# Softmax transposes of an attention stage as two 64-row halves in place of one 128-row block

## Chip, cores and metric

The kernel runs on one core of a Trainium2 chip. The metric is device time in microseconds (us), the median of repeated executions. Engines are named as the profile names them: PE is TensorE's matmul, PEld its weight load, DVE VectorE, ACT ScalarE, POOL GpSimd, SP SyncE.

## The reference

One layer of an encoder trunk, sequence length 1024, width 1024, all in float32. Cut to what matters here:

```python
hn = rmsnorm(h, norm_mix_g); z = hn @ w_in
u, (q, k, v) = z[..., :512], jnp.split(z[..., 512:], 3, axis=-1)   # 8 heads of 64
a = pool_mixer(u, pool_w, pool_b, pool_scale)
o = chunk_attention(q, k, v, rel_bias)       # own chunk of 64 and the 8 before it
h = h + jnp.concatenate([a, o], -1) @ w_out
# then a gated MLP with a causal convolution (d_ff 2816), a gated per-layer embedding, a last rmsnorm

# inside chunk_attention, for one chunk of 64 queries
s = jnp.einsum('bqhd,bkhd->bhqk', qb, kb) * scale + bias
pr = jax.nn.softmax(jnp.where(valid, s, -inf), axis=-1)
out = jnp.einsum('bhqk,bkhd->bqhd', pr, vb)
```

## The kernel before

Every large product is made of three matmuls on halves of a float32 number (`mm3`, lines 126 to 130: high by high, high by low, low by high); `split` (lines 132 to 134) makes the halves with one ACT copy and one DVE subtraction. These products fill almost the whole program.

The attention stage handles 64 tiles `i`, 8 heads by 8 blocks of 128 queries. A block sees `nk` blocks of 128 keys: 1, 2, 3, 4 and then 5 for the last four blocks of a head, so the stage has 8 x (1+2+3+4+4x5) = 240 blocks of probabilities. For each tile:

- `scores(i)` (lines 333 to 361): scores on PE into banks 4 and 5 of PSUM; DVE adds the bias and finds the row extreme (L346 for five blocks, L354 for fewer); ACT takes the exponential with a row sum (L356); DVE takes the reciprocal (L357); ACT (L359) or DVE (L361) scales. The probabilities stand in `S`, in tile `F`, queries on the partitions, float32.
- `probs_t(i)` (lines 363 to 378), two tiles later: the `nk` blocks of `S` are transposed on PE (L370) so that keys stand on the partitions. The results go to PSUM banks 6 and 7 (`pst`), from which ACT writes the high half (L377) and DVE the low half (L378) to the tile `PT`, which lies in `B`. There is one `pst`: the first transpose of a tile waits until L378 of the tile before has read it.
- `values` (lines 380 to 394), every second tile: probabilities by values (L387, L388) and their evacuation (L393, L394).

A transpose here loads the block of `S` as the array's weights (LDWEIGHTS, stationary) and streams the identity `ident` through it (MATMUL, moving): the output block has as many columns as the moving operand.

PE's order is the order in which the code is written. Between the attention's own matmuls the loop puts steps of a generator `rest()`: one `mm3` of the input projections of later heads and of the pooling part. `fill_room` and `credit` set how many such steps go to each tile. The order on DVE and ACT is set by a scheduler by priorities; the evacuations L377 and L378 are asked for early (`tc.high_priority(AHEAD)`).

The stage runs from about 60 us to 282 us of the span; the first and last L370 start at 60.5 and 268.5 us. Output projection, MLP and the rest follow.

Of the kernel before, what the change touches and what calls it, by code (L numbers as in the profile page):

```python
# [11 lines left out]
P = 128  # L12
# [5 lines left out]
HD = 64  # L18
# [75 lines left out]
def trunk(tc, xT, pT, vecs, w_qk0, w_in, w_v, bias, counts, pool_w, w_out, w_up, w_down,  # L94
          w_gate, w_ple, out):
    nc = tc.nc
    act, dve, pe, pool, sp = nc.scalar, nc.vector, nc.tensor, nc.gpsimd, nc.sync

    with tc.tile_pool(name="sb", bufs=1) as sb, \
# [7 lines left out]
        ident = sb.tile([P, P], F32, name="ident")  # L107
        PS = pp.tile([P, 8, 512], F32, name="PS")
# [6 lines left out]
        def r(kb, n):  # L115
            if kb >= 128:
                return B[:, int((kb - 128) * KW):int((kb - 128) * KW) + n]
            return R[:, int(kb * KW):int(kb * KW) + n]
# [4 lines left out]
        def rv(ap):  # L123
            return ap.bitcast(F32)
# [203 lines left out]
        def keys(i):  # L328
            t = i % NTOK
            k0 = max(0, t - 4)  # L330
            return i // NTOK, t, k0, t + 1 - k0
# [31 lines left out]
        def probs_t(i):  # L363
            h, t, k0, nk = keys(i)
            S = Sb[i % 3]
            w = i // 2
            pt = PT[w % 2]
            pst = PS[:, 6:8].rearrange("p a b -> p (a b)")[:, 0:nk * P]
            for j in range(nk):
                pe.transpose(pst[:, j * P:(j + 1) * P], S[:, j * P:(j + 1) * P], ident)  # L370
            pst = pst.rearrange("p (k q) -> p k q", k=nk)
            i0 = k0 - (t // 2 * 2 - 4)
            qs = slice(t % 2 * P, (t % 2 + 1) * P)
            hi = pt[:, 0, i0:i0 + nk, qs]
            lo = pt[:, 1, i0:i0 + nk, qs]
            with tc.high_priority(AHEAD):
                act.activation(hi, pst, AF.Copy)  # L377
                dve.tensor_tensor(lo, pst, rv(hi), ALU.subtract)  # L378
# [162 lines left out]
        for i in range(NI + 3):  # L541
            if i < NI:
                h, t, k0, nk = keys(i)
# [15 lines left out]
            for z in range(n_):  # L559
                if due and z >= n_ // 2:  # L560
                    probs_t(i - 2)
                    due = False
                if next(fill, True) is False:
                    break
                credit -= 1
            if due:
                probs_t(i - 2)
# [189 lines left out]
        for z, d in enumerate((0, 4, 1, 5, 2, 6, 3, 7)):  # L757
            k = z // 2
# [297 lines left out]
        pt = [[(r(b, 512), r(b + 2, 512)) for b in (96 + 16 * h, 104 + 16 * h)] for h in range(2)]  # L1056
# [238 lines left out]
```

## Time and profile before

| | |
|---|---|
| median of 3 runs | 1137.39 us (1137.12 to 1137.82) |
| the profiled execution's own time | 1137.53 us |
| its span, first to last instruction | 1135.8 us |
| granted TensorE clock, mean | 0.998 of full speed |
| PE busy in the span | 99% |
| DVE, ACT busy in the span | 78%, 53% |
| transposes L370 | 240 matmuls, 240 weight loads |

Rows of a timeline give the start, the length, the engine, the line, the operation and what it writes and reads; runs of the same instruction are merged with a count. TensorE's matmuls overlap, and a row's length is longer than the distance to the next start; the work of one is best read from that distance. In rows of groups the numbers behind the bar are the group's total busy time in us, the mean of one in ns, and the idle time of the engine before them.

### The profile page before, as it was taken

What the parts mean: (1) busy time and instruction counts of PE and PEld (TensorE: products, weight loads), DVE (VectorE), ACT (ScalarE), POOL (GpSimd) and SP (SyncE); (2) the same over time, 40 slices, a digit from 0 to 9 for tenths busy, and PEclk for the clock granted to TensorE, in tenths of its full rate; (3) what the DMA queues carried; (4) which work ended last, traced back from release to release, by engine and by line L of the source; (5) the groups of instructions that cost most, each with busy time, mean ns of one, the idle gap of its engine ahead of it and who ended that gap; (6) DMA issues with size and microseconds to landing.
All of it is one profiled execution on the core that took longest, in us unless ns stands there. A gap on an engine that the chain in (4) does not pass through costs nothing.

```text
span 1135.8 us, 15750 instructions
## 1 busy us (share of the span) xinstructions
PE 1126.1 (99%) x5675; PEld 956.0 (84%) x5675; DVE 891.0 (78%) x1546; ACT 604.5 (53%) x1071; POOL 143.1 (13%) x188
## 2 busy tenths in 40 slices
PE   9999999999999999999999999999999999999997
PEld 7988998888888888888888888888888888888897
DVE  7678878779658888887788778877887789986854
ACT  8568677765654554444444444444444444674544
POOL 0000000074002200120112011201120112000000
PEclk9999999999999999999999999999999999999999
DMA  7110102103600154575557555755575556420012
GB/s 267 38 50 31 49 13 68 40 29 131 194 19 10 57 151 135 139 174 142 137 155 178 143 130 162 176 145 131 159 171 151 130 152 129 147 93 19 1 75 75
DMA packets 64446, 124.84 MB, mean 110 GB/s; under 512 B 7280, under 2 KB 8560, under 8 KB 64368
## 3 DMA queue, kind: packets, MB, share of 16 engines
q1 hardware_dynamic: 50400, 98.60, 25.9%
q0 software_dynamic: 13824, 25.17, 13.6%
q8 instruction: 44, 0.72, 0.3%
q14 instruction: 34, 0.28, 0.1%
q10 hardware_dynamic: 144, 0.07, 0.0%
HBM read 109.13 MB, written 14.68 MB: 109 GB/s over the span
## 4 chain that ended last, share of the span: by engine, by line
PE 92%; DVE 3%; issue 2%; ACT 1%; POOL 1%; DMA 0%; SPq 0%; POOLq 0%; DVEq 0%; ACTq 0%
PE PS L128 28%; PE PS L129 28%; PE PS L130 28%; PE PS L370 2%; PE PS L388 1%; PE PS L387 1%; DVE R L134 1%; PE PS L345 1%; PE PS L344 1%; ACT R L133 1%; DMA F<-in_w_qk 0%; PE PS L353 0%; PE PS L352 0%; POOL TB L778 0%; DVE F L760 0%
## 5 line engine op out<-in xcount | busy, mean ns | idle before, releaser
L128 PE MATMUL PS<-R 128*128 128x512 f32 (+1 forms) x1176 | 442.7, 376 | 0.2 <-ACT R L232 0.2
L130 PE MATMUL PS<-R 128*128 128x512 f32 (+1 forms) x1176 | 437.8, 372 | 0.0
L129 PE MATMUL PS<-R 128*128 128x512 f32 (+1 forms) x1112 | 420.1, 378 | 0.3 <-DVE R L233 0.3
L130 PEld LDWEIGHTS PS<-R 128*128 128x128 f32 x1176 | 221.7, 188 | 39.0
L128 PEld LDWEIGHTS PS<-R 128*128 128x128 f32 x1176 | 221.8, 189 | 37.8 <-ACT R L232 0.6
L129 PEld LDWEIGHTS PS<-R 128*128 128x128 f32 x1112 | 209.7, 189 | 37.0 <-DVE R L233 0.8
L133 ACT ACTIVATE R<-F 128x512 fp32r<-128x512 f32 (+2 forms) x225 | 140.6, 637 | 173.9 <-PE PS L129 75.2
L134 DVE TENSOR_TENSOR R<-F,R 128x512 fp32r<-128x512 f32 (+2 forms) x221 | 152.8, 701 | 48.3 <-ACT R L133 47.5
L1013 DVE TENSOR_TENSOR F<-F,PS 128x512 f32<-128x512 f32 x140 | 92.6, 682 | 5.8 <-PE PS L130 5.6
L133 ACT ACTIVATE BQ<-RW 128x512 fp32r<-128x512 f32 x90 | 52.6, 622 | 81.1 <-PE PS L129 77.1
L703 DVE TENSOR_TENSOR F<-F 128x512 f32<-128x512 f32 x88 | 60.7, 689 | 39.0 <-DMA F<-in_w_up 37.2
L956 POOL DMA_DIRECT2D RW<-Yd x56 | 49.0, 875 | 260.3 <-DMA RW<-Yd 201.4
L956 POOL DMA_DIRECT2D RW<-in_w_down x40 | 35.5, 941 | 233.5 <-DMA RW<-in_w_down 189.7
L134 DVE TENSOR_TENSOR BQ<-RW,BQ 128x512 fp32r<-128x512 f32 x90 | 59.2, 687 | 1.8 <-PE PS L129 1.3
L356 ACT ACTIVATE F<-F,small 128x640 f32<-128x640 f32 (+2 forms) x64 | 44.4, 693 | 21.3 <-DVE small L354 13.2
L129 PE MATMUL PS<-BQ 128*128 128x512 f32 x140 | 54.6, 390 | 0.1
L130 PE MATMUL PS<-BQ 128*128 128x512 f32 x140 | 54.5, 389 | 0.0
L128 PE MATMUL PS<-R,BQ 128*128 128x512 f32 x140 | 54.5, 389 | 0.0
L128 PE MATMUL PS<-BQ 128*128 128x512 f32 x140 | 54.5, 389 | 0.0
L129 PE MATMUL PS<-R,BQ 128*128 128x512 f32 x140 | 54.5, 389 | 0.0
L130 PE MATMUL PS<-R,BQ 128*128 128x512 f32 x140 | 54.5, 389 | 0.0
L839 ACT ACTIVATE F<-F,vec 128x1024 f32<-128x1024 f32 (+1 forms) x25 | 28.6, 1143 | 44.2 <-DVE F L814 40.8
(188 smaller groups left out, 1806.3 us busy)
## 6 DMA issues: line engine op xcount, KB each, us to landing
F<-in_w_up SPq DMA_DIRECT2D x91, 256.0 KB, 4.0
RW<-Yd SPq DMA_DIRECT2D x60, 256.0 KB, 3.7
RW<-Yd POOLq DMA_DIRECT2D x56, 256.0 KB, 4.8
RW<-in_w_down SPq DMA_DIRECT2D x50, 256.0 KB, 2.8
RW<-in_w_down POOLq DMA_DIRECT2D x40, 256.0 KB, 6.0
Yd<-F SPq DMA_DIRECT2D x40, 256.0 KB, 3.1
F<-in_w_in SPq DMA_DIRECT2D x10, 512.0 KB, 3.7
F<-in_xT SPq DMA_DIRECT2D x16, 256.0 KB, 5.8
```

Source lines behind the costliest of these rows:

```text
L128: pe.matmul(ps, ahi, bhi, start=first, stop=False, skip_group_check=more)
L129: pe.matmul(ps, ahi, blo, start=False, stop=False, skip_group_check=more)
L130: pe.matmul(ps, alo, bhi, start=False, stop=last, skip_group_check=more)
L133: both = (act.activation(hi, src, AF.Copy), dve.tensor_tensor(lo, src, rv(hi), ALU.subtract))
L134: dve.tensor_tensor(lo, src, rv(hi), ALU.subtract))
L344: pe.matmul(PS[:, 4 + z, 0:320], q, K2[:, ks], start=True, stop=False)
L356: act.activation(S[:, 0:n], S[:, 0:n], AF.Exp, bias=s_[:, 0:1], scale=-1.0, accum_out=s_[:, 1:2])
L370: pe.transpose(pst[:, j * P:(j + 1) * P], S[:, j * P:(j + 1) * P], ident)
L703: return dve.tensor_tensor(rawu[to], rawu[a], rawu[b], op)
L839: act.activation(y, Gb[:, 2 + a:2 + b], AF.Identity, bias=vec[:, C_CB + fi:C_CB + fi + 1], scale=cw(2))
L956: pool.dma_start(t, src, accum_op=ALU.add)
L1013: dve.tensor_tensor(t, t, PS[:, 4 + d], ALU.subtract if n in (1, 5) else ALU.add)
```

## The change

Each transpose of 128 queries by 128 keys becomes two of 64 queries by 128 keys. The first takes partitions 0 to 63 of `S` and the upper left quarter of `ident` and stands on the upper 64 rows of the array; the second takes partitions 64 to 127 and the lower right quarter and stands on the lower 64 rows (`tile_position`). Each writes 64 columns instead of 128, the first to bank 6 and the second to bank 7. The two evacuations read both banks in turns of 64 columns and write the same places as before.

```diff
-            pst = PS[:, 6:8].rearrange("p a b -> p (a b)")[:, 0:nk * P]
             for j in range(nk):
-                pe.transpose(pst[:, j * P:(j + 1) * P], S[:, j * P:(j + 1) * P], ident)
-            pst = pst.rearrange("p (k q) -> p k q", k=nk)
+                for x in range(2):
+                    rows = slice(HD * x, HD * x + HD)
+                    pe.transpose(PS[:, 6 + x, j * HD:(j + 1) * HD], S[rows, j * P:(j + 1) * P], ident[rows, rows],
+                                 tile_position=(HD * x, 0))
+            pst = PS[:, 6:8, 0:nk * HD].rearrange("p a (k q) -> p k a q", k=nk)
             i0 = k0 - (t // 2 * 2 - 4)
             qs = slice(t % 2 * P, (t % 2 + 1) * P)
-            hi = pt[:, 0, i0:i0 + nk, qs]
-            lo = pt[:, 1, i0:i0 + nk, qs]
+            hi, lo = [pt[:, x, i0:i0 + nk, qs].rearrange("p k (a q) -> p k a q", a=2) for x in range(2)]
             with tc.high_priority(AHEAD):
                 act.activation(hi, pst, AF.Copy)
                 dve.tensor_tensor(lo, pst, rv(hi), ALU.subtract)
```

HD is 64 and P is 128. From the second added line on the new kernel's lines stand one lower than before: the transposes are L371, the evacuations L378 and L379.

PE, at a tile of five key blocks in the middle of the stage, before (PS is PSUM; L128 to L130 are the three matmuls of `mm3`, L387 and L388 those of `values`):

```order
L129 MATMUL PS<-R 128x512
L130 MATMUL PS<-R 128x512
L370 MATMUL PS<-ident,F 128x128 x5
L128 MATMUL PS<-R 128x512
L129 MATMUL PS<-R 128x512
L130 MATMUL PS<-R 128x512
L387 MATMUL PS<-B,R 128x256
```

The same place of PE after:

```order
L129 MATMUL PS<-R 128x512
L130 MATMUL PS<-R 128x512
L371 MATMUL PS<-ident,F 128x64 x10
L128 MATMUL PS<-R 128x512
L129 MATMUL PS<-R 128x512
L130 MATMUL PS<-R 128x512
L388 MATMUL PS<-B,R 128x256
```

Five transposes have become ten with half the columns, in the same place between the same matmuls. This holds for all 64 tiles, and nothing else on PE moves.

ACT, at the tiles around 105 us, before (L359 scales the probabilities, L377 is the evacuation, L356 the exponential of a next tile, L133 the high halves of a weight):

```order
L324 ACTIVATE F<-F 128x640
L359 ACTIVATE F<-F,small 128x640
L377 ACTIVATE B<-PS 128x5x128
L356 ACTIVATE F,small<-F,small 128x128
L133 ACTIVATE R<-F 128x512 x2
L356 ACTIVATE F,small<-F,small 128x256
```

The same place of ACT after:

```order
L324 ACTIVATE F<-F 128x640
L359 ACTIVATE F<-F,small 128x640
L356 ACTIVATE F,small<-F,small 128x128
L378 ACTIVATE B<-PS 128x5x128
L133 ACTIVATE R<-F 128x512 x2
L356 ACTIVATE F,small<-F,small 128x256
```

One evacuation has moved behind one exponential. There are a few such swaps of neighbours on ACT and DVE in the whole program.

## Prediction

> **What bounds the kernel now.** I read the page's shares first, then the chain that ended last, then the attention stage by itself.
>
> ```profile
> span 1135.8 us, 15750 instructions
> PE 1126.1 (99%) x5675; PEld 956.0 (84%) x5675; DVE 891.0 (78%) x1546; ACT 604.5 (53%) x1071; POOL 143.1 (13%) x188
> ...
> PE 92%; DVE 3%; issue 2%; ACT 1%; POOL 1%; DMA 0%; SPq 0%; POOLq 0%; DVEq 0%; ACTq 0%
> PE PS L128 28%; PE PS L129 28%; PE PS L130 28%; PE PS L370 2%; PE PS L388 1%; PE PS L387 1%; DVE R L134 1%; PE PS L345 1%; PE PS L344 1%; ACT R L133 1%; DMA F<-in_w_qk 0%; PE PS L353 0%; PE PS L352 0%; POOL TB L778 0%; DVE F L760 0%
> ```
>
> PE is 92% of the chain, and the transposes L370 stand in it with 2% of their own, some 23 us. The stage in which they lie, by engine (busy us, with counts, then the granted clock):
>
> ```profile
> core 0: us, PE busy (x) PEld busy (x) DVE busy (x) ACT busy (x) POOL busy (x), PEclk, DMA share, GB/s
> ...
> 60.00:282.00 222.00, 221.11 (x1373) 195.48 (x1372) 181.23 (x430) 154.20 (x327) 35.16 (x62) 1.00 0.15 50
> ```
>
> In these 222 us PE is idle 0.9 us, DVE 41 us, ACT 68 us. A busy PE row need not be PE at its peak, so the waits around L370 follow (total us, times, longest), and then L370 itself:
>
> ```profile
> ACT B L377 <- PE PS L370: 15.4, 13, 1.8
> DVE B L378 <- ACT B L377: 8.5, 18, 1.2
> PEld PS L370 <- DVE B L378: 4.2, 10, 0.8
> PE PS L370 <- DVE B L378: 0.8, 2, 0.5
> ...
> L370 PEld LDWEIGHTS PS<-ident,F x240: 137/140/145, 60.2 to 268.4; 128*128 128x128 f32 x120
> L370 PE MATMUL PS<-ident,F x240: 270/272/329, 60.5 to 268.5; 128*128 128x128 f32 x120
> ```
>
> PE waits for the free `pst` 12 times, 5.0 us in all. Everything else in the stage goes at PE's pace, so PE time added to or taken from a transpose group is time of the kernel, nearly one for one.
>
> **What a group costs now.** A tile of one key block, then one of five, on PE:
>
> ```profile
> 110.92 0.39 PE L130 MATMUL PS<-R 128*128 128x512 f32 x1
> 111.15 0.27 PE L370 MATMUL PS<-ident,F 128*128 128x128 f32 x1
> 111.17 0.47 PE L128 MATMUL PS<-R,B 128*128 128x512 f32 x1
> 111.49 0.39 PE L129 MATMUL PS<-R,B 128*128 128x512 f32 x1
> ...
> 103.38 0.40 PE L130 MATMUL PS<-R 128*128 128x512 f32 x1
> 103.62 0.71 PE L370 MATMUL PS<-ident,F 128*128 128x128 f32 x5
> 104.08 0.48 PE L128 MATMUL PS<-R 128*128 128x512 f32 x1
> 104.40 0.40 PE L129 MATMUL PS<-R 128*128 128x512 f32 x1
> ```
>
> From L130 to L129 it is 0.57 us with one transpose and 1.02 us with five, so 0.45/4 = 0.11 us for each. Finer: five take 0.71 us, the last one's length is 0.272, and (0.711-0.272)/4 = 0.109 us. Two whole 512-column matmuls at 0.23 us and one transpose at 0.109 make the 0.57: going from the matmuls to transposes and back costs nothing of its own. A group of n costs n x 0.109 us; all cost 240 x 0.109 = 26.2 us.
>
> Is that step the load or the stream? The loads of the same group of five, then the loads and matmuls of a group that had waited, with the longest matmul of that group in ns:
>
> ```profile
> 103.39 0.70 PEld L370 LDWEIGHTS PS<-ident,F 128*128 128x128 f32 x5
> 104.06 0.19 PEld L128 LDWEIGHTS PS<-R 128*128 128x128 f32 x1
> 104.17 0.19 PEld L129 LDWEIGHTS PS<-R 128*128 128x128 f32 x1
> ...
> 106.67 0.53 PEld L370 LDWEIGHTS PS<-ident,F 128*128 128x128 f32 x5 [0.45 <-DVE B L378]
> 106.67 0.77 PE L370 MATMUL PS<-ident,F 128*128 128x128 f32 x5
> ...
> L370 PE MATMUL PS<-ident,F x1: 329/329/329, 106.7 to 106.7; 128*128 128x128 f32 x1
> ```
>
> A load starts when the matmul before it takes over the weights that were loaded before. After the wait nothing streams, and five loads span 0.53 us, of which the last one's length is 0.14: the four distances make 0.39 = 3 x 0.109 + 0.06. So the first load needed only 0.058 us (the first matmul's 329 ns against 272 says the same, 57 ns), and the steps of 0.109 after it are the stream of 128 columns. The load of the ordinary matmul L128 takes 0.11 us (104.06 to 104.17), hidden today exactly behind the last transpose's stream. The Trainium skill ("TensorE: Matmul & The Clock Gate", section "LDWEIGHTS (loading the stationary operand)") has a load take its columns divided by 1.2 per ns, 107 ns for 128 columns. The ordinary load's 0.11 us agrees; the transpose's 0.058 us does not, and the measurement decides; by the page's price the forecast's sum below would be 240 x 0.049 = 11.8 us higher.
>
> **The change part by part.** Loads double to 480, each of the same 128 columns, so 0.058 us each: bounds 0.029 (by the rows it fills) and 0.058; I take 0.058, since the columns stay. The streams double to 480 of 64 columns: half of 0.109, 0.055 us each, if the stream goes by columns as it does for 128; the other end is 0.109, a fixed time.
>
> Two halves on different rows of the array can run at the same time. Then a pair steps by the longer of load and stream, 0.058 us in place of 0.109. If they follow one another, a pair takes 2 x 0.058 = 0.116. No row shows it, as every instruction in the trace uses 128 rows. I take the overlap, because a load already runs beside another block's stream throughout this trace, and the halves share neither rows nor bank.
>
> The tail grows: L128's load, 0.109, used to fit behind a stream of 0.109 and now has a last stream of 0.055 to hide behind.
>
> Going from the whole array to its halves and back is new, twice in each of 64 groups. The free change of kind above bounds its price from below at 0. From above: a 512-column matmul lasts 0.40 us and the next starts 0.24 after it, so what is still in flight is 0.16 us. If the array must be empty before it is divided, each side costs d between 0 and 0.16; I take the middle, 0.08, as neither row is a division. The first half's load (0.058) then no longer hides behind L130, nor L128's behind the last stream.
>
> The sum, with handover: per group d + n x 0.058 + 0.055 + d + 0.109. Over all: 240 x 0.058 = 13.9, and 64 x (0.16 + 0.055 + 0.109) = 20.7; together 34.6 against 26.2 now, +8.4 us (d = 0: -1.8; d = 0.16: +18.6).
>
> The evacuations read PSUM in pieces of 64 columns. Nearest rows, for 640 and 256 columns in pieces of 128 and for 256 columns in four pieces of 64:
>
> ```profile
> L377 ACT ACTIVATE B<-PS 128x640 fp32r<-128x640 f32 x32 | 22.2, 693 | 7.8 <-PE PS L370 7.5
> L377 ACT ACTIVATE B<-PS 128x256 fp32r<-128x256 f32 x8 | 3.0, 380 | 3.6 <-PE PS L370 3.2 <-DVE F L446 0.3
> L259 ACT ACTIVATE R<-PS,small 128x256 fp32r<-128x256 f32 x9 | 4.2, 466 | 1.5 <-PE PS L130 1.5
> L378 DVE TENSOR_TENSOR B<-PS,B 128x640 fp32r<-128x640 f32 x32 | 26.3, 823 | 6.0 <-ACT B L377 5.5
> L378 DVE TENSOR_TENSOR B<-PS,B 128x256 fp32r<-128x256 f32 x8 | 3.4, 423 | 0.2
> L260 DVE SCALAR_TENSOR_TENSOR R<-PS,small,R 128x256 fp32r<-128x256 f32 x9 | 4.3, 480 | 0.1
> ```
>
> If all of 466-380 and 480-423 came from the pieces, that is 22 ns a piece on ACT and 14 on DVE; 240 more pieces make 5.2 and 3.4 us. They carry a scale by row as well, so I take nothing. The idle 68 and 41 us cover either; uncovered it would be at most 8.6 us. Nothing suggests a gain.
>
> Of the scheduler's swaps I cost the one shown above. It stands ahead of the wait of 0.45 us at 106.67:
>
> ```profile
> 105.05 0.69 ACT L377 ACTIVATE B<-PS 128x640 fp32r<-128x640 f32 x1
> 105.64 0.39 ACT L356 ACTIVATE F<-F,small 128x128 f32<-128x128 f32 x1
> 105.79 0.82 DVE L378 TENSOR_TENSOR B<-PS,B 128x640 fp32r<-128x640 f32 x1
> ```
>
> The evacuation now queues behind that exponential; L378 and PE's next group come up to 0.6 us later. Against that, each of the 12 waits shrinks when PE's work between them grows by 0.13 us a group (8.4/64): 12 x 0.13 = 1.6. Net -1.0. Forecast: 1137.5 (the profiled execution's time, 0.1 above the median) + 8.4 - 1.0 = 1144.9 us.
>
> **Rivals.** *Overlap without handover (faster).* The divided array needs no emptying, as the other change of kind needs none; the first load stays behind L130. Per group (n-1) x 0.058 + 0.109: 176 x 0.058 + 64 x 0.109 = 17.2 us, -9.0: 1128.5 us. For it: 0.57 = 2 x 0.23 + 0.109. Against: no row with a divided array. It decides as long as both handovers of a group cost under 9.0/64 = 0.14 us together.
>
> *The halves do not overlap.* PE takes them in order, the second load starting when the first half streams. Per group (2n-1) x 0.058 + 0.109: 416 x 0.058 + 7.0 = 31.1, +4.9: 1142.4 us. For it: in every row above a load starts only as the matmul ahead of it takes over. With the handover it is 480 x 0.058 + 20.7 = 48.5, +22.3: 1159.8 (d = 0.16: 1170).
>
> *A half costs what a whole did.* The 0.109 is a fixed time: 480 x 0.109 = 52.3, +26.1: 1163.6 us. Against: the 0.058 above.
>
> Of the handover the Trainium skill ("TensorEngine Tiling (Array Packing)", section "Key Properties") says that a change of tiling mode drains TensorE. No row here shows it; it speaks for the forecast and against the faster rival.
>
> **Numbers.** Chances: overlap with handover 0.34, overlap without 0.30, in order without 0.17, in order with 0.11, fixed time 0.08. A measurement of this kernel tells 0.2%, 2.3 us, from no change. Faster: 0.30 and the cheap end of the forecast, 0.32; same 0.06; slower 0.62. The forecast's own range is 1135 to 1156 (d from 0 to 0.16). To leave out no more than 2 in 10 the range takes in the faster rival with 1.5 us for its waits, 1127, and the in-order handover to its middle, 1161.
>
> **What would show it.** In the new profile: pairs of L371 in a group step by about 0.06 us for two (overlap) or 0.12 (in order); L130 to the first L371 in a group grows from 0.23 to about 0.37, and from the last L371 to L129 from 0.34 to about 0.48 (handover). If L130 to the first L371 stays at 0.23, the forecast is wrong by that step; if the halves keep 0.109 each, by the stream. ACT and DVE rows of 640 columns should stay near 693 and 823 ns, and idle PE before L371 under 5 us.

## The result and the profile after

The changed kernel takes 1146.39 us (1146.04 to 1147.27) against 1137.36 us: 9.0 us more, ratio 1.0077 (95% interval 1.0065 to 1.0089). Its profiled span is 1144.5 us. The page of the changed kernel, engines and then the chain that ended last:

```profile
span 1144.5 us, 16230 instructions
PE 1133.4 (99%) x5915; PEld 948.5 (83%) x5915; DVE 893.0 (78%) x1546; ACT 605.4 (53%) x1071; POOL 143.1 (13%) x188
...
PE 95%; issue 2%; ACT 2%; DVE 1%; DMA 0%; SPq 0%; POOL 0%; POOLq 0%; DVEq 0%; ACTq 0%
```

PE has 240 more matmuls and 240 more loads; the load rows nevertheless add up to 7.5 us less, and DVE and ACT do as much as before. The chain is PE still more than it was. The groups of the transposes and of their two evacuations in the changed kernel:

```profile
L371 PE MATMUL PS<-ident,F 64*128 64x64 f32 x480 | 28.5, 235 | 0.7 <-DVE B L379 0.6
L379 DVE TENSOR_TENSOR B<-PS,B 128x640 fp32r<-128x640 f32 x32 | 26.3, 822 | 6.8 <-ACT B L378 6.3
L378 ACT ACTIVATE B<-PS 128x640 fp32r<-128x640 f32 x32 | 22.2, 694 | 8.4 <-PE PS L371 8.2
L371 PEld LDWEIGHTS PS<-ident,F 64*128 64x128 f32 x480 | 19.8, 138 | 21.5 <-issue 8.6 <-DVE B L379 3.6 <-DVE F L395 3.3
```

The evacuations take 694 and 822 ns against 693 and 823: reading two banks in pieces of 64 columns costs nothing. By busy time, in which overlapping rows count once, the transposes got cheaper: 28.5 us for all halves against 37.1 for the whole ones, whose row before is this:

```profile
L370 PE MATMUL PS<-ident,F 128*128 128x128 f32 x240 | 37.1, 274 | 0.9 <-DVE B L378 0.8
```

The busy rows thus point the wrong way; the distances between starts show the cost. On PE in the changed kernel, a tile of five key blocks, then one of one block:

```profile
105.38 0.39 PE L130 MATMUL PS<-R 128*128 128x512 f32 x1
105.70 0.52 PE L371 MATMUL PS<-ident,F 64*128 64x64 f32 x10
106.15 0.50 PE L128 MATMUL PS<-R 128*128 128x512 f32 x1
106.48 0.39 PE L129 MATMUL PS<-R 128*128 128x512 f32 x1
...
113.36 0.40 PE L130 MATMUL PS<-R 128*128 128x512 f32 x1
113.69 0.28 PE L371 MATMUL PS<-ident,F 64*128 64x64 f32 x2
113.89 0.50 PE L128 MATMUL PS<-R,B 128*128 128x512 f32 x1
114.23 0.39 PE L129 MATMUL PS<-R,B 128*128 128x512 f32 x1
```

The loads around the group of five, and the lengths of its ten halves (minimum, median and maximum in ns):

```profile
105.16 0.19 PEld L130 LDWEIGHTS PS<-R 128*128 128x128 f32 x1
105.70 0.39 PEld L371 LDWEIGHTS PS<-ident,F 64*128 64x128 f32 x10 [0.35 <-DVE B L379]
106.15 0.19 PEld L128 LDWEIGHTS PS<-R 128*128 128x128 f32 x1
106.26 0.19 PEld L129 LDWEIGHTS PS<-R 128*128 128x128 f32 x1
...
L371 PE MATMUL PS<-ident,F x10: 221/222/272, 105.7 to 106.0; 64*128 64x64 f32 x10
```

- **Inside a group** the gain is there: ten halves take 0.52 us where five whole transposes took 0.71. The starts in the trace lie 3 to 4 ns apart within a pair and 61 ns from pair to pair, after a first step of 111 ns.
- **Going in**: from L130 to the first half it is 0.32 us, where it was 0.23, so 0.09 for the handover. The first half's load starts only then (before, it started with L130's stream), and the first half is 272 ns long against 222: 0.05 us of load that nothing hides.
- **Coming out**: the last half starts at 105.70 + 0.52 - 0.22 = 106.00, and L128's load at 106.15. That is 0.15 us. With the half's stream taken as 0.055, half of a whole one's 0.109, another 0.095 is left for the handover. Then comes the load's 0.11 with nothing beside it.

From L130 to L129 a group of five takes 1.10 us (1.02 before) and a group of one 0.87 (0.57 before). Over the trace the extra of a group, by medians, is 0.30 us with one block, 0.24 with two, 0.20, 0.15, and 0.10 with five: a fixed 0.35 less 0.05 for each block. With 8, 8, 8, 8 and 32 groups that makes 8 x 0.89 + 32 x 0.10 = 10.3 us.

There is a trap in the waits of the changed kernel:

```profile
PEld PS L371 <- issue: 8.6, 24, 0.4
PEld PS L371 <- DVE B L379: 3.6, 8, 0.9
PEld PS L371 <- DVE F L395: 3.3, 9, 0.4
PEld PS L371 <- DVE small L354: 1.5, 4, 0.4
```

These look like waits for DVE. Most are 0.35 us long and stand in nearly every group, whatever is named: they are L130's stream and the handover, put down to whichever semaphore came last. In only three groups did PE really wait for L379: there the first half starts within 0.06 us of its end, later than usual by 0.52, 0.24 and 0.18 us, 0.9 in all. In the kernel before there are nine such groups with 1.9 us in all. The longest of the three is the place where the scheduler had moved an evacuation behind an exponential:

```profile
108.34 0.40 PE L130 MATMUL PS<-R 128*128 128x512 f32 x1
109.18 0.53 PE L371 MATMUL PS<-ident,F 64*128 64x64 f32 x10 [0.44 <-DVE B L379]
```

Here L130 to L371 is 0.84 us, 0.52 over the usual 0.32; before, the same group waited 0.17 over its 0.23.

### The profile page after: what moved, and what is told of

The parts are those of the page before. It is cut to its first block, busy times and chain, and to the rows that moved or that the text cites. A ratio compares the mean times of both kernels' runs of the same rounds, so it can differ in the third digit from the quotient of the medians.

```text
span 1144.5 us, 16230 instructions
## 1 busy us (share of the span) xinstructions
PE 1133.4 (99%) x5915; PEld 948.5 (83%) x5915; DVE 893.0 (78%) x1546; ACT 605.4 (53%) x1071; POOL 143.1 (13%) x188
## 4 chain that ended last, share of the span: by engine, by line
PE 95%; issue 2%; ACT 2%; DVE 1%; DMA 0%; SPq 0%; POOL 0%; POOLq 0%; DVEq 0%; ACTq 0%
PE PS L128 30%; PE PS L129 29%; PE PS L130 29%; PE PS L371 2%; PE PS L388 1%; PE PS L389 1%; PE PS L344 1%; PE PS L345 1%; DMA F<-in_w_qk 0%; PE PS L352 0%; PE PS L353 0%; PE PS L621 0%; ACT F L356 0%; ACT R L281 0%; ACT R L279 0%
## 5 line engine op out<-in xcount | busy, mean ns | idle before, releaser
L128 PE MATMUL PS<-R 128*128 128x512 f32 (+1 forms) x1176 | 442.9, 377 | 1.7 <-ACT F L791 0.9
L130 PE MATMUL PS<-R 128*128 128x512 f32 (+1 forms) x1176 | 437.4, 372 | 0.0
L129 PE MATMUL PS<-R 128*128 128x512 f32 (+1 forms) x1112 | 419.6, 377 | 0.5 <-DVE R L233 0.5
L128 PEld LDWEIGHTS PS<-R 128*128 128x128 f32 x1176 | 221.5, 188 | 41.1 <-ACT F L791 1.3
L130 PEld LDWEIGHTS PS<-R 128*128 128x128 f32 x1176 | 221.4, 188 | 39.0
L129 PEld LDWEIGHTS PS<-R 128*128 128x128 f32 x1112 | 209.4, 188 | 37.0 <-DVE R L233 1.2
L133 ACT ACTIVATE R<-F 128x512 fp32r<-128x512 f32 (+2 forms) x225 | 140.7, 637 | 172.9 <-PE PS L129 81.4
L133 ACT ACTIVATE BQ<-RW 128x512 fp32r<-128x512 f32 x90 | 52.6, 622 | 81.1 <-PE PS L129 77.0
L356 ACT ACTIVATE F<-F,small 128x640 f32<-128x640 f32 (+2 forms) x64 | 44.3, 693 | 22.7 <-DVE small L354 13.7
L129 PE MATMUL PS<-BQ 128*128 128x512 f32 x140 | 54.6, 390 | 0.1
L130 PE MATMUL PS<-BQ 128*128 128x512 f32 x140 | 54.5, 389 | 0.0
L129 PE MATMUL PS<-R,BQ 128*128 128x512 f32 x140 | 54.5, 389 | 0.0
L130 PE MATMUL PS<-R,BQ 128*128 128x512 f32 x140 | 54.5, 389 | 0.0
L128 PE MATMUL PS<-R,BQ 128*128 128x512 f32 x140 | 54.5, 389 | 0.0
L128 PE MATMUL PS<-BQ 128*128 128x512 f32 x140 | 54.5, 389 | 0.0
```

What stands on the lines that cost most here:

```text
L128: pe.matmul(ps, ahi, bhi, start=first, stop=False, skip_group_check=more)
L129: pe.matmul(ps, ahi, blo, start=False, stop=False, skip_group_check=more)
L130: pe.matmul(ps, alo, bhi, start=False, stop=last, skip_group_check=more)
L133: both = (act.activation(hi, src, AF.Copy), dve.tensor_tensor(lo, src, rv(hi), ALU.subtract))
L356: act.activation(S[:, 0:n], S[:, 0:n], AF.Exp, bias=s_[:, 0:1], scale=-1.0, accum_out=s_[:, 1:2])
```

## Experiments

The theory: a gain per block (two halves at once) and a fixed price per group, for dividing the array and undoing it. The rivals: the price goes by the number of small instructions, or the halves do not really run together.

**One half, alone, ahead of whole transposes.** Everything else as before:

```diff
+            pe.transpose(PS[:, 7, 384:448], S[0:HD, 0:P], ident[0:HD, 0:HD], tile_position=(0, 0))
             for j in range(nk):
                 pe.transpose(pst[:, j * P:(j + 1) * P], S[:, j * P:(j + 1) * P], ident)
```

> The kernel before with one extra 64-row transpose (upper rows of the first block, into unused columns of bank 7, never read) ahead of each of the 64 groups of whole transposes. Handover theory (dividing the array and undoing it costs by itself): per group entry 0.089 + exposed load 0.055 + stream 0.055 + exit 0.097 + exposed load of the next transpose 0.058 = 0.354 us, 64 of them 22.7 us: 1160 us. Rival (the cost goes by the number of halves, as small matmuls with their own loads): 64 x 0.058 = 3.7 us: 1141 us.

and its control:

```diff
+            pe.transpose(PS[:, 7, 384:512], S[:, 0:P], ident)
             for j in range(nk):
                 pe.transpose(pst[:, j * P:(j + 1) * P], S[:, j * P:(j + 1) * P], ident)
```

> The control: the same extra instruction at the same place as a whole 128-row transpose (into unused columns of bank 7, never read). Both theories: 64 x 0.109 = 7.0 us more than before: 1144.4 us, so less than the 64-row one if the handover theory holds, and more than it if not.

Measured beside a kernel before of 1138.25 us: 1157.29 with the half (ratio 1.0167, 1.0151 to 1.0182) and 1144.90 with the whole (1.0058, 1.0043 to 1.0073). The smaller instruction costs 19.0 us, the larger 6.7. PE with the half ahead, a group of five:

```profile
80.13 0.39 PE L130 MATMUL PS<-R,B 128*128 128x512 f32 x1
80.45 0.27 PE L369 MATMUL PS<-ident,F 64*128 64x64 f32 x1
80.65 0.76 PE L371 MATMUL PS<-ident,F 128*128 128x128 f32 x5
81.17 0.48 PE L128 MATMUL PS<-R,B 128*128 128x512 f32 x1
81.49 0.40 PE L129 MATMUL PS<-R,B 128*128 128x512 f32 x1
```

The same 0.32 on the way in, 0.20 from the half to the whole ones, and a first whole transpose that again shows its load (five take 0.76 instead of 0.71). From L130 to L129 it is 1.36 us, 0.34 more than before and close to the expected 0.354; 64 of them are 21.8 us, and the kernel got 19.0. Of the missing 2.8 us some 1.7 are shorter waits for the one `pst`: groups that start right behind L378 of the tile before lost 1.9 us in the kernel before, and with the half ahead (where that line is L379) 0.2. The rest was not followed. So the price is one of going between whole-array and half-array instructions, not of their number. No run has 64-row instructions that leave the array undivided, so these two are not told apart, and the rows do not show what PE does in the 0.09 us of a handover.

**All upper halves first, then all lower ones:**

```diff
-            for j in range(nk):
-                for x in range(2):
+            for x in range(2):
+                for j in range(nk):
```

> The changed kernel with all upper halves of a tile first and then all lower halves. If the gain inside a group comes from two neighbours on different rows running together, it goes: 240 x 0.060 less one shared step in each of 64 groups, 176 x 0.060 = 10.6 us more than the changed kernel: 1157 us. Rival (the rows of the array work off their halves independently of the order, or the pairs never ran together): 1146 us.

Measured: 1150.13 us (ratio to before 1.0103, 1.0088 to 1.0118), 3.7 above the changed kernel's 1146.39: neither the 10.6 nor the 0. (The two were measured beside kernels before of 1138.25 and 1137.36; as differences to these they lie 2.9 apart.) The order on PE, three upper and three lower halves and then five and five:

```profile
92.47 0.41 PE L371 MATMUL PS<-ident,F 64*128 64x64 f32 x6
...
79.33 0.64 PE L371 MATMUL PS<-ident,F 64*128 64x64 f32 x10
```

and in the changed kernel, where they alternate, for three blocks:

```profile
92.22 0.40 PE L371 MATMUL PS<-ident,F 64*128 64x64 f32 x6
```

Six halves take 0.41 us against 0.40: although written one after the other, they still ran in pairs, 10 ns apart, so a lower half started before upper halves that stand ahead of it in the program. Ten take 0.64 against 0.52, which is two steps of 0.06: by the starts in the trace the lower halves fell two steps behind, and the last two of them ran alone. The rows do not name upper and lower, but the lengths do. The first half on its rows has a load that nothing hides and lasts 272 ns; in an alternated group both of the first pair do. In the group of five and five these are the first and the third to start. The first three starts are:

```profile
L371 PE MATMUL PS<-ident,F x3: 223/272/272, 79.3 to 79.4; 64*128 64x64 f32 x3
```

So the first lower half, sixth in the program, started third. 32 groups x 0.12 = 3.8 us accounts for the difference; the groups of the two traces, from L130 to L129, sum to 67.7 and 64.1 us. My expectation missed since it took PE to work off its matmuls strictly in order. That the overlap is real stands all the firmer: a group that loses the overlap at two steps is longer by two steps.

**Halves only where there are five blocks.** The change's loop, `pst`, `hi` and `lo` stand in the first branch, those of before in the second:

```diff
+            if nk == BANDT:
...
+            else:
...
```

> Halves only in the 32 tiles of five key blocks, whole transposes in the other 32. Handover theory, a fixed price of 0.35 us a group less 0.050 us a block: a group of five costs 0.098 us more than before, 32 of them 3.1 us: 1140.5 us. Rival (the change's 9.0 us go by blocks): 160/240 of 9.0 = 6.0 us: 1143.4 us.

Measured: 1140.42 us beside 1138.25 (ratio 1.0024, 1.0014 to 1.0033), 2.2 us more. This fits the fixed price (3.1), not one by blocks (6.0). It is better than the changed kernel and still not as good as the one before.

**Longer groups.** Every transpose of a group done twice over, in both kernels:

```diff
-            for j in range(nk):
+            for j in 2 * list(range(nk)):
```

> The kernel before with every transpose of a group done twice over, into the same places (twice the work, groups of 2 to 10). Both theories: 240 x 0.109 = 26.2 us more than before: 1163.5 us.

> The changed kernel with every pair of halves done twice over, into the same places. Handover theory: the handovers are paid once, the 240 added pairs step by 0.061 us: 14.6 us more than the changed kernel, 1161.0 us, now below the whole transposes done twice (1163.5). Rival (halves cost more than whole ones in proportion): the change's 9.0 us double, 1163.5 + 18.0 = 1181.5 us.

Measured beside 1137.63: 1165.91 us whole (1165.62 to 1168.51) and 1166.64 halves (1164.85 to 1168.88). The change's 9.0 us have shrunk to nothing that these spreads tell, far from a doubling to 18. The halves missed their expected 1161.0 by 5.6 us. About half of that is waiting for the one `pst`: by the starts behind L379, 3.8 us against 0.9 in the changed kernel. In the traces a doubled group of five takes less in halves, 1.43 us against 1.56 from L130 to L129, but in the kernel's time the crossing was not shown: inconclusive on that. So three times over, `3 * list(range(nk))`:

> The kernel before with every transpose done three times over (groups of 3 to 15). Both theories: 2 x 26.2 = 52.4 us more than before, by the run with two about 2 us more in waits: 1190 to 1192 us.

> The changed kernel with every pair of halves done three times over. Handover theory: 480 added pairs at 0.061 to 0.064 us, 29 to 31 us more than the changed kernel, by the run with two up to 10 us more in waits: 1176 to 1187 us, clear below the whole transposes done three times. If halves cost as much as whole ones once groups are long (as the medians of the two runs with two could be read): the same 1190 to 1192 us.

Measured beside 1137.31: 1189.85 us whole (ratio 1.046, 1.0443 to 1.0477) and 1180.83 halves (1.0381, 1.0365 to 1.0396). Now the halves are faster by 9.0 us. A group of five blocks three times over, whole and then halves, in the two kernels' timelines of PE:

```profile
84.26 1.80 PE L370 MATMUL PS<-ident,F 128*128 128x128 f32 x15
```

```profile
86.25 1.15 PE L371 MATMUL PS<-ident,F 64*128 64x64 f32 x30
```

(1.80 - 0.71)/10 = 0.109 us for a whole one, (1.15 - 0.52)/10 = 0.063 for a pair. The kernel gained less than the groups: 480 added pairs at 0.063 are 30 us, and it took 34.4 more than the changed kernel. Most of the rest is waiting for the one `pst`. These waits of the kernel with halves three times over have it in them:

```profile
PEld PS L371 <- DVE B L379: 9.6, 17, 1.2
PEld PS L371 <- issue: 6.5, 18, 0.4
PE PS L371 <- DVE B L379: 3.1, 6, 0.8
```

The trap is in these rows too: 0.35 us of each load's wait is stream and handover. By the starts right behind L379, PE really waited in 11 groups, 4.2 us over the usual distance, against 0.9 in the changed kernel.

No version tried beats the kernel before. With the groups that this kernel has, one to five blocks, halves would need more than 0.35/0.05 = 7 blocks in a group to pay.

## Why the prediction was right

The forecast was 1144.9 us, overlap with handover; measured 1146.4. The mechanism was as told; that the time came within 1.5 us was in part luck, since the largest unknown, the handover, was put at the middle of its bounds without a row for it.

- **What binds a whole transpose**: the stream of 0.109, not the load of 0.058. Confirmed: with as many columns to load and half as many to stream, pairs step by 0.061 in place of 0.109. The first half's load lays open 0.05 (272 against 222 ns). Whether the load or the stream of 0.055 sets the 0.061 is not told apart.
- **Overlap of the halves**: taken without a row of its own; confirmed by starts 3 to 4 ns apart and by the order experiment. One after the other, pairs would have stepped by 0.116.
- **Handover**: the term with the widest bounds, 0 to 0.16 a side. It measured 0.09 going in and 0.095 coming out; the middle, 0.08, was a little low, 64 x 0.025 = 1.6 us. The Trainium skill's rule that a change of tiling mode drains TensorE ("TensorEngine Tiling (Array Packing)", section "Key Properties") agrees with these 0.09 us on each side; it gives no time for it. Of the signs named, the way out grew from 0.34 to 0.48 us as forecast; the way in grew to 0.32 in place of 0.37, because the load of 0.05 stands inside the first half's row.
- **Loads that lose their cover**: 0.05 in front and 0.11 behind, as written. The changes of kind that are free in the kernel before, ordinary matmul to whole transpose and back, told nothing of this one.
- **Sum without waits**: +8.4 forecast, +10.3 by the groups. The missing 1.9 are mostly the handover's 1.6. The 176 steps between pairs at 0.061 add 0.5, the first load at 0.05 in place of 0.058 takes 0.5 back, and the rest is rounding.
- **Waits**: -1.0 forecast. The groups from L130 to L129, waits included, sum to 64.1 us after and 55.3 before, +8.7, so waits gave back about 1.6. By the starts behind L378, only nine of the 12 waits that were counted on held PE up, as a load may wait while L130 still streams. The nine lost 1.9 us and laid open 9 x 0.057 of load, 2.4 together; after, three groups wait and lose 0.9. The moved evacuation did lengthen its wait, by 0.35 us, not the 0.6 allowed.
- **Evacuations**: nothing, as taken.

The faster rival, overlap without handover, failed at its own condition: both handovers together cost 0.185 us a group with the loads they lay open on top, against the 0.14 that it could bear.

## What to carry to other kernels

Ask of each small matmul whether its load or its stream sets its step, from the distances between starts and not from busy time. Here the stream did, and two halves on different rows gained; a case where the load sets it was not run. Dividing the array is paid once for each stretch (here 0.35 us, of which 0.19 for the handovers and the rest for loads that lose their cover), so gather enough divided work in one stretch, here more than seven blocks, before it pays. A cost that is fixed per stretch and a gain that goes by pieces are told apart by making the stretches longer, even with useless work.

## What the runs showed that was not expected

PE started 64-row matmuls of the lower rows ahead of earlier ones on the upper rows: three and three written in sequence took 0.41 us, nearly as when alternated (0.40), while five and five lost two steps (0.64 against 0.52). Four and four still paired throughout (1.058 us from L130 to L129 against 1.051). In both cases the first lower half started ahead of three upper ones that stand before it; in no run did it pass four. The Trainium skill ("TensorE: Matmul & The Clock Gate", section "Part 3: Packing small matmuls — row/col tiling") has matmuls start strictly in program order; here they did not, and the measurement decides. Its 4 ns between starts on different rows agrees with the 3 to 4 ns seen.
